# One decoder layer on one core: the order of the queues is made from another simulator's times

## The chip, the core and the metric

The kernel runs on one core of a Trainium2 chip. The metric is the device time of one execution in microseconds (us); the median of three runs is compared. TensorE (PE in the rows) multiplies matrices, VectorE (DVE), ScalarE (ACT) and GpSimd (POOL) do element work, and SyncE (SP) issues most of the DMAs. Each engine works through its own queue of instructions in a fixed order and stops where an instruction's operands are not ready.

## The reference, cut to what matters

1024 prompt positions and 8 single decode positions (1032 columns) go through one layer of width 1024:

```python
h = _rmsnorm(x, p['norm_mix'])
proj = h @ p['w_in']                          # 1024 -> 1792 + 768 + 512 + 3072 columns
z, q, k, v, xq, gates = jnp.split(proj, IN_SPLITS, axis=-1)
out_a, S_new = _rwkv_branch(z, z_prev, S0, p) # a recurrence over the positions
out_b = _sink_attn(...)                       # sliding window, 8 heads
out_c = _mem_attn(xqh, mem_k, mem_v)          # cross-attention, 4 heads
g = jax.nn.sigmoid(gates)                     # three gates of 1024 columns
merged = g0 * (out_a @ w_br_a) + g1 * (out_b @ w_br_b) + g2 * (out_c @ w_br_c)
x = x + merged @ p['w_out']
h2 = _rmsnorm(x, p['norm_ffn'])
x = x + jnp.square(jax.nn.relu(h2 @ p['w_up'])) @ p['w_down']
```

## The kernel before

**Dense products.** All of it is float32. A product is made from high and low parts by three matmuls for each 128 rows of the contraction (`dense`, L181 to L183). `in_proj` computes one block of 128 columns of `proj`: it loads the weights (L163, a tile `wst`), splits them on ACT (L173) and POOL (L174), and runs 24 matmuls into each of three banks named `mm` (384, 384 and 264 columns), 72 in all. ACT takes each bank out. Of these blocks 24 belong to the gates: `gates` puts a tanh on the bank (L286, tile `gt`) and stores it (L287). Below, *a dense matmul* is one of these 128x128 matmuls into an `mm` bank.

**The recurrence** is cut into 8 units, u0 to u7 (`unit`, a generator of three stages). Stage 1 makes the factors of a later unit (among them L479 and L496, small sums on PE). Stage 2 makes the tile `GM` (L545) and solves a triangular system in 62 short DVE operations (L581, L583), 31 after each other. Stage 3 takes the solution (L597, L600) and does four steps, each one a chain across engines: PE L616 and L619, ACT L622, PE L626, ACT L627, PE L629, DVE L631 (the new state), which the next L616 reads. PE's L633 lies beside it. u0 starts its first step at the first L616.

**What stands around the units.** The source puts dense blocks between the stages:

```python
FILL = [lambda: pair_proj(2), lambda: pair_proj(3)] + [lambda i=i: gates((2, 2, 2, 2, 2)[i]) for i in range(5)]
for u in range(7):
    next(units[u + 1])
    if u == 0:
        FILL[0]()
    flush(units[u])
    next(units[u + 1])
    if u:
        FILL[u]()
```

Behind u7 come the cross-attention (16 pieces; first PE row is a `cp` bank from `mkTh`), the keys of the sliding window (L995), 32 pieces of sliding-window attention (`qunit`, L1092 to L1128), the last gates (`gates(24)`, L1257), then the branch products with `w_br_c`, `w_br_a` and `w_br_b` (first row: an `mm` bank from `oh`), the output product, the second norm (about 1345 to 1410 us) and the MLP (`stream`, L1555).

**What sets the order.** The source order is not the queues' order. When the block of the `tile.TileContext` ends, the framework's scheduler goes through the program with a simulator's times, and at each point gives an engine one of the instructions that are ready by those times. Its result is a fixed order for each engine's queue, and with it which tile takes which buffer. Nothing is reordered on the chip by the program itself.

## Time and profile before

| | |
|---|---|
| median of 3 runs | 2059.64 us (2055.43 to 2061.08) |
| the profiled execution | 2062.78 us, its span 2061.0 us |
| mean granted TensorE clock | 0.948 of full speed |
| busy share of the span | PE 94%, PE's weight loads 89%, DVE 65%, ACT 37%, POOL 29% |

The profiled execution is one of its own, beside the three timed runs. The span is from its first to its last instruction. Busy shares are means over stages that have different limits.

### The profile page before, as it was taken

To read this page: it belongs to the slowest core of one execution; us is meant where nothing else is said; L and a number is where in the kernel's file an instruction comes from. 1 tells how busy PE (TensorE), PEld (TensorE's weight loads), DVE (VectorE), ACT (ScalarE), POOL (GpSimd) and SP (SyncE) were. 2 spreads that over 40 slices of the span, in tenths; PEclk is the share of its full clock that TensorE was granted. 3 is DMA by queue.
4 is the path that set the end of the run, shared out by engine and by line. 5 is a ranking of instruction groups with operands and counts; after the bars stand their busy time and mean duration, and the time that the engine had idled before them with its cause. 6 is when DMAs were issued, how large, how long until landed. Compare 5 with 4: busy or idle time off the path is not lost. (4 is left out here: it accounts for less than half of the span.)

```text
span 2061.0 us, 36994 instructions
## 1 busy us (share of the span) xinstructions
PE 1928.9 (94%) x14079; PEld 1834.5 (89%) x14079; DVE 1344.0 (65%) x3247; ACT 755.8 (37%) x1617; POOL 590.7 (29%) x606
## 2 busy tenths in 40 slices
PE   4989999998999989999989999979999998999998
PEld 4879888887888888989979999969999998999997
DVE  7465667576676457477652575687666669788864
ACT  4432323232322335344652123343333344344433
POOL 3422211111111135322020000146655554344421
PEclk9999788799898999999999999989999999999999
DMA  4544322323232145232236346416544448455413
GB/s 142 169 152 130 88 73 80 90 80 93 60 84 70 30 129 168 85 95 79 65 112 212 109 142 206 123 49 197 166 150 137 149 150 288 126 148 159 141 40 101
DMA packets 257104, 250.69 MB, mean 122 GB/s; under 512 B 43102, under 2 KB 204959, under 8 KB 256927
## 3 DMA queue, kind: packets, MB, share of 16 engines
q1 hardware_dynamic: 254656, 241.24, 38.5%
q0 software_dynamic: 2016, 6.53, 1.0%
q8 instruction: 111, 1.82, 0.4%
q14 instruction: 67, 0.54, 0.1%
q10 hardware_dynamic: 254, 0.55, 0.1%
HBM read 174.19 MB, written 74.46 MB: 121 GB/s over the span
## 5 line engine op out<-in xcount | busy, mean ns | idle before, releaser
L181 PE MATMUL mm<-hh,wh 128*128 128x384 f32 (+1 forms) x1152 | 391.7, 340 | 5.7 <-ACT z L342 5.1
L182 PE MATMUL mm<-hl,wh 128*128 128x384 f32 (+1 forms) x1152 | 390.0, 339 | 7.3 <-DVE hl L217 7.3
L183 PE MATMUL mm<-hh,wl 128*128 128x384 f32 (+1 forms) x1152 | 390.5, 339 | 1.3 <-POOL wl L174 1.3
L1555 PE MATMUL z<-h,wl 128*128 128x258 f32 x1488 | 265.6, 287 | 7.9 <-DVE x L1648 4.5
L1555 PE MATMUL z<-h,wh 128*128 128x258 f32 x1488 | 263.2, 285 | 8.1 <-DVE wh L1310 4.9
L182 PEld LDWEIGHTS mm<-hl,wh 128*128 128x128 f32 x1152 | 227.6, 198 | 11.3 <-DVE hl L217 8.2
L181 PEld LDWEIGHTS mm<-hh,wh 128*128 128x128 f32 x1152 | 228.5, 198 | 10.1 <-ACT z L342 5.6
L183 PEld LDWEIGHTS mm<-hh,wl 128*128 128x128 f32 x1152 | 228.3, 198 | 5.1 <-POOL wl L174 1.7
L1555 PEld LDWEIGHTS z<-h,wl 128*128 128x128 f32 x1488 | 217.6, 193 | 9.8 <-ACT wl L1536 5.0
L1555 PEld LDWEIGHTS z<-h,wh 128*128 128x128 f32 x1488 | 216.1, 192 | 9.2 <-DVE wh L1310 5.1
L174 POOL TENSOR_TENSOR wl<-wst,wh 128x1024 fp32r<-128x1024 f32 x48 | 116.9, 2435 | 215.6 <-ACT wh L173 211.1
L1648 DVE TENSOR_TENSOR x<-z,x 128x516 f32<-128x516 f32 x168 | 115.9, 691 | 68.8 <-PE z L1555 65.5
L1555 PE MATMUL z<-l,wl 128*128 128x258 f32 x744 | 154.7, 288 | 3.1 <-DVE l L1310 3.1
L1555 PE MATMUL z<-l,wh 128*128 128x258 f32 x744 | 153.5, 286 | 1.0 <-DVE l L1310 1.0
L173 ACT ACTIVATE wh<-wst 128x1024 fp32r<-128x1024 f32 x84 | 88.8, 1057 | 141.4 <-PE mm L182 75.0
L1555 PEld LDWEIGHTS z<-l,wl 128*128 128x128 f32 x744 | 117.9, 192 | 3.7 <-DVE l L1310 3.6
L1555 PEld LDWEIGHTS z<-l,wh 128*128 128x128 f32 x744 | 117.0, 191 | 1.7 <-DVE l L1310 1.7
L1503 POOL TENSOR_TENSOR sw<-wst 128x256 f32<-128x256 f32 (+1 forms) x56 | 55.1, 984 | 208.0 <-DMA wst<-in_w_down 87.9
L1607 POOL TENSOR_TENSOR us<-us,us 128x516 f32<-128x516 f32 x64 | 96.5, 1519 | 52.0 <-issue 22.1
L1310 DVE TENSOR_TENSOR l<-ub,h 128x516 fp32r<-128x516 f32 (+1 forms) x120 | 92.9, 800 | 6.3 <-ACT h L1335 6.1
L183 PE MATMUL mm<-oh,wl 128*128 128x384 f32 (+1 forms) x288 | 92.2, 320 | 0.0
L182 PE MATMUL mm<-ol,wh 128*128 128x384 f32 (+1 forms) x288 | 92.1, 320 | 0.0
(510 smaller groups left out, 4281.1 us busy)
## 6 DMA issues: line engine op xcount, KB each, us to landing
u<-us SPq DMA_DIRECT2D x112, 258.0 KB
ub<-u SPq DMA_DIRECT2D x112, 258.0 KB
wst<-in_w_in SPq DMA_DIRECT2D x48, 512.0 KB
wst<-in_w_down SPq DMA_DIRECT2D x24, 512.0 KB
gate<-gt SPq DMA_DIRECT2D x48, 192.0 KB
gl<-gate SPq DMA_DIRECT2D x16, 516.0 KB
wst<-in_w_out SPq DMA_DIRECT2D x16, 512.0 KB
wst<-in_w_up SPq DMA_DIRECT2D x16, 512.0 KB
```

The source lines that it names most:

```text
L173: A.activation(hi, st, AF.Copy)
L174: last_lo[:] = [eng.tensor_tensor(lo, st, hi.bitcast(F32), ALU.subtract)]
L181: PE.matmul(out, lhsT=wh, rhs=xh, start=first and k == 0, stop=False)
L182: PE.matmul(out, lhsT=wh, rhs=xl, start=False, stop=False)
L183: end = PE.matmul(out, lhsT=wl, rhs=xh, start=False, stop=last and k == n - 1)
L1310: V.tensor_tensor(lo, x, hi.bitcast(F32), ALU.subtract)
L1503: G.tensor_tensor(s[:, k:k + n], v, w, op)
L1555: op = PE.matmul(z[:, s, :HQ], lhsT=t[:, a, k], rhs=right[ks[k], s, i][b], start=go and k + q == 0, stop=q == 2 and k == nk - 1, skip_grou ...
L1607: G.tensor_tensor(t, x, y, ALU.subtract)
L1648: V.tensor_tensor(c, z, c, ALU.add)
```

## The change

One argument is added where the context is opened. No instruction, operand, pool or line of the kernel's body changes; the framework's scheduler now takes the durations from its other simulator when it orders the queues.

```diff
@@ -1761,7 +1761,7 @@
-    with tile.TileContext(nc) as tc:
+    with tile.TileContext(nc, schedule_with_timeline_sim=True) as tc:
         tile_step(tc, ins, outs)
```

The orders differ over most of the kernel. Three places stand here. The first is PE's queue at the first step of u4. `cp` and `sm` banks belong to the units, `mm` banks are dense blocks. Before:

```order
L616 MATMUL cp_4699<-st_129_601,BR_4037 128x128
L616 MATMUL cp_4699<-st_131_603,BR_4037 128x128
L619 MATMUL cp_4699<-UV_4279,GM_4249 64x64 x4
L183 MATMUL mm_5692<-hh_8_79,wl_5633 128x264
L181 MATMUL mm_5692<-hh_8_79,wh_5632 128x264
L182 MATMUL mm_5692<-hl_9_80,wh_5632 128x264
L183 MATMUL mm_5692<-hh_8_79,wl_5633 128x264
L626 MATMUL cp_4708<-pt_4706,GM_4249 64x64 x4
```

After, at the same step:

```order
L616 MATMUL cp_4699<-st_129_601,BR_4037 128x128
L616 MATMUL cp_4699<-st_131_603,BR_4037 128x128
L619 MATMUL cp_4699<-UV_4279,GM_4249 64x64 x4
L501 MATMUL sm_5262<-c_ident_69,sn_5237 20x128
L626 MATMUL cp_4708<-pt_4706,GM_4249 64x64 x4
L629 MATMUL cp_4708<-UV_4279,CKT_4278 64x64 x4
L633 MATMUL cp_4699<-UV_4279,GM_4249 64x64 x4
L616 MATMUL cp_4727<-st_130_602,BR_4037 128x128
```

The dense matmuls that stood between the step's parts are gone: units u3, u4, u5 and three steps of u6 stand without any. They have moved to earlier units. The second place is PE's queue after the change at the first step of u1:

```order
L600 MATMUL cp_2688<-Y_2676,XW_2480 64x64 x8
L616 MATMUL cp_2700<-st_125_597,BR_1954 128x128
L616 MATMUL cp_2700<-st_127_599,BR_1954 128x128
L619 MATMUL cp_2700<-UV_2460,GM_2430 64x64 x4
L182 MATMUL mm_4522<-hl_7_78,wh_4490 128x384
L183 MATMUL mm_4522<-hh_6_77,wl_4491 128x384
L181 MATMUL mm_4522<-hh_6_77,wh_4490 128x384
```

Of such dense rows 22 follow here before the next row of the step (L626), where three or four stood before the change. Counted over the whole queue, the dense matmuls that stand between two marks are:

| from, to (first row of each) | before | after |
|---|---|---|
| L479 of u0, first step of u0 | 217 | 265 |
| u0, u1 | 138 | 287 |
| u1, u2 | 161 | 306 |
| u2, u3 | 133 | 308 |
| u3, u4 | 157 | 0 |
| u4, u5 | 132 | 0 |
| u5, u6 | 172 | 0 |
| u6, u7 | 93 | 144 |
| u7, first cross-attention row | 323 | 364 |
| cross-attention, L995 | 310 | 209 |
| L995, first `qunit` | 239 | 183 |
| `qunit` pieces and the last gates, to the branch products | 697 | 684 |

Up to the branch products both orders have had the same dense matmuls. Before the first step of u0 the order after has 70 more behind it (22 of them ahead of u0's L479). Nine `qunit` pieces late in their stage have no dense matmul among them after the change, and the last gates stand among the last pieces, where before they stood behind them.

The third place is SP's queue, where the branch products' first weights are loaded. Before:

```order
L287 DMA gate_553<-gt_11464 128x384
L1274 DMA tot_1793_11250<-gate_553 128x1032
L163 DMA wst_11637<-in_w_br_c 128x4x256
L287 DMA gate_553<-gt_11492 128x384
L163 DMA wst_11729<-in_w_br_c 128x4x256
L287 DMA gate_553<-gt_11520 128x264
```

After:

```order
L1274 DMA tot_1794_11251<-gate_553 128x1032
L287 DMA gate_553<-gt_11582 128x384
L163 DMA wst_11637<-in_w_br_c 128x4x256
L163 DMA wst_11729<-in_w_br_c 128x4x256
L287 DMA gate_553<-gt_11610 128x264
L1274 DMA tot_1795_11252<-gate_553 128x1032
```

The load now stands behind four more stores of gate banks; one store of a gate is left behind it, where five were left before. In the MLP the orders are close to each other; loads of `in_w_up` stand behind the loads of `u` there, and the first load of `in_w_out` behind loads of `x`.

## Rows read from the trace of the kernel before

**Rows 1.** The page: busy times; TensorE's clock, in tenths, in 40 slices of the span.

```profile
PE 1928.9 (94%) x14079; PEld 1834.5 (89%) x14079; DVE 1344.0 (65%) x3247; ACT 755.8 (37%) x1617; POOL 590.7 (29%) x606
PEclk9999788799898999999999999989999999999999
```

**Rows 2.** Busy time by stretch: before u0, the qunits, the MLP.

```profile
core 0: us, PE busy (x) PEld busy (x) DVE busy (x) ACT busy (x) POOL busy (x), PEclk, DMA share, GB/s
182.00:281.85 99.85, 87.15 (x514) 80.83 (x513) 67.81 (x196) 27.78 (x54) 20.89 (x30) 0.86 0.36 104
892.00:1115.00 223.00, 208.79 (x1410) 198.21 (x1411) 134.80 (x417) 114.67 (x323) 40.92 (x68) 0.93 0.38 116
1410.00:2061.00 651.00, 635.27 (x5225) 631.45 (x5223) 462.91 (x702) 247.38 (x496) 299.55 (x277) 0.99 0.48 150
```

**Rows 3.** The same for u0 to u7, each from first L616 on, and the cross-attention.

```profile
281.85:339.26 57.41, 56.62 (x394) 49.41 (x393) 40.70 (x149) 18.35 (x45) 8.23 (x10) 0.82 0.28 79
339.26:407.50 68.24, 64.54 (x429) 57.29 (x427) 42.84 (x183) 19.91 (x44) 9.13 (x15) 0.80 0.29 80
407.50:460.43 52.93, 51.37 (x388) 44.32 (x387) 37.80 (x149) 16.66 (x38) 7.26 (x8) 0.90 0.29 79
460.43:523.50 63.07, 57.25 (x419) 49.69 (x417) 41.62 (x173) 19.22 (x43) 7.26 (x8) 0.89 0.31 84
523.50:576.93 53.43, 52.39 (x391) 45.38 (x391) 36.03 (x150) 17.53 (x44) 7.35 (x7) 0.90 0.31 82
576.93:632.48 55.55, 51.26 (x411) 45.86 (x409) 37.52 (x152) 15.12 (x33) 9.01 (x10) 0.94 0.30 81
632.48:668.67 36.19, 35.92 (x294) 31.24 (x293) 25.17 (x107) 12.07 (x26) 5.14 (x4) 0.90 0.19 49
668.67:749.25 80.58, 75.61 (x541) 71.43 (x539) 29.19 (x111) 24.71 (x50) 11.88 (x12) 0.96 0.19 56
749.25:842.70 93.45, 84.55 (x573) 78.68 (x571) 63.19 (x137) 43.69 (x118) 45.30 (x34) 0.98 0.55 165
```

**Rows 4.** The `mm` instructions alone in four of those stretches, and in 1080 to 1110.

```profile
281.85:339.26 57.41, 32.71 (x138) 25.45 (x138) 0.00 (x0) 2.75 (x6) 0.82 0.28 79
460.43:523.50 63.07, 33.13 (x157) 26.49 (x157) 0.00 (x0) 3.23 (x7) 0.89 0.31 84
632.48:668.67 36.19, 20.38 (x93) 14.96 (x93) 0.00 (x0) 3.18 (x7) 0.90 0.19 49
668.67:749.25 80.58, 60.20 (x323) 53.25 (x323) 0.00 (x0) 10.09 (x23) 0.96 0.19 56
...
1080.00:1110.00 30.00, 30.00 (x197) 30.00 (x195) 0.00 (x0) 3.20 (x7) 1.00 0.82 270
```

**Rows 5.** Timeline, the first step of u3: start, duration, engine, line, tiles.

```profile
460.43 0.71 PE L616 MATMUL cp<-st,BR 128*128 128x128 f32 x4
...
463.73 0.45 PE L629 MATMUL cp<-UV,CKT 128*64 128x64 f32 x8
...
464.31 1.18 DVE L631 SCALAR_TENSOR_TENSOR st<-st,gc,cp 64x64 f32<-64x64 f32 x4 [0.62 <-PE cp L629]
```

**Rows 6.** Timeline, the first step of u4.

```profile
523.50 1.22 PE L616 MATMUL cp<-st,BR 128*128 128x128 f32 x4
...
529.91 1.18 DVE L631 SCALAR_TENSOR_TENSOR st<-st,gc,cp 64x64 f32<-64x64 f32 x4 [3.24 <-PE cp L629]
```

**Rows 7.** Waits, 339 to 577 us: total us, times, longest.

```profile
DVE sn L481 <- PE sm L479: 22.5, 4, 6.7
DVE st L631 <- PE cp L629: 13.9, 10, 3.2
DVE xt L581 <- DMA AT<-amat: 7.7, 2, 4.4
```

**Rows 8.** Timeline, SP's first load of `w_br_c` and the first branch row on PE.

```profile
1106.91 0.38 SPq L163 DMA_DIRECT2D wst<-in_w_br_c  x1
...
1119.50 0.33 PE L181 MATMUL mm<-oh,wh 128*128 128x384 f32 x1
```

## The prediction

> **What bounds the kernel now.** I read the page first: PE is busy for 94% of the span and no other engine for more than 65% [rows 1]. So the kernel is PE's queue, and time can come or go in three ways only: dense work, which is the same before and after, stalls of PE, and stretches at the lower clock. The clock line of the page says where to look: the slices at 7 and 8 tenths lie from the first norm to the end of the units [rows 1]. I then cut the span into stages. From 1410 us on PE is busy for 635.27 of 651.00 us at a mean granted clock of 0.99: little to win [rows 2]. The `qunit` stage is busy for 208.79 of 223.00 us, at 0.93 [rows 2]. The units run at 0.80 to 0.94 and PE has idle time in most of them [rows 3].
>
> Third, the price of a dense matmul. Where nothing else runs (1080 to 1110 us, clock 1.00), 197 of them take 30.00 us, 0.152 us each [rows 4]. In u0 PE spends 32.71 us on 138 of them, 0.237 us each, and in the stretch from u7 on 60.20 us on 323, 0.186 us each [rows 4]: beside a recurrence step the same instruction is dearer, since it runs partly at half clock. PE's remaining work in a unit is its busy time less that of the `mm` rows: 56.62 - 32.71 = 23.9 us in u0, 57.25 - 33.13 = 24.1 in u3, and, with no later unit to prepare, 35.92 - 20.38 = 15.5 in u6 and 75.61 - 60.20 = 15.4 in u7 [rows 3, 4].
>
> Fourth, what a step of the recurrence takes. u3's first runs from L616 at 460.43 to the end of L631 at 464.31 + 1.18 = 465.49: 5.06 us, with L616 at 0.71 us for four rows, the level of 2.4 GHz [rows 5]. u4's first runs from 523.50 to 531.09: 7.59 us, and the same four rows take 1.22, the level of 1.2 GHz [rows 6]. DVE follows the chain and solves the next unit's triangle in between: 41.62, 36.03 and 37.52 us busy in u3, u4, u5 [rows 3].
>
> **The change part by part.** The instructions are the same, so every term is an amount of dense work at another place, plus what that place then waits for.
>
> *Before u0.* 70 more dense matmuls stand ahead of u0's first step, 70 x 0.152 = 10.6 us. PE was idle for 99.85 - 87.15 = 12.7 us there, and the clock was 0.86 [rows 2], so that they can fit into gaps: 0, with 0 to +11.
>
> *u0 to u3.* The order now has 287 + 306 + 308 = 901 dense matmuls there, in groups of some 22 between the parts of a step, 3.3 us of cover for a hand-over that needs less. PE should not wait, nor the clock fall: 901 x 0.152 = 137 us, plus 3 x 25 us of its own (24 measured, one for breaks) = 212 us. Before, the three took 57.41 + 68.24 + 52.93 = 178.6 [rows 3]. Term: +33. With own work of 22 us, as it would be wholly at the higher clock, +24; at u7's 0.186 us for a dense matmul, 901 x 0.186 + 75 = 243, +64.
>
> *u3 to u6.* No dense matmul stands there. A unit then takes what DVE and the chain take. Lower bound: DVE's own 38.4 us (the mean of the three), plus its waits in the rows for four units, 13.9 / 4 = 3.5 for L631 and 7.7 / 4 = 1.9 for the loaded triangle, and about 3 of the 22.5 / 4 = 5.6 for L479, which had dense rows ahead of it [rows 7]: 47 us. That holds while the clock is high. At the lower level each of four steps takes 7.59 - 5.06 = 2.53 us more [rows 5, 6], 10 together, and the other PE rows a little: 58 us. The units of before, with three dense rows in a gap, had 0.89, 0.90 and 0.94 [rows 3], so that both levels will occur; I take the middle, 52. u5's recurrence prepares less for what follows, 46. So 52 + 52 + 46 = 150, against 63.07 + 53.43 + 55.55 = 172.1 [rows 3]: -22 (47 gives -37, 58 gives -4).
>
> *u6 to u7.* 51 more dense matmuls, 7.8 us, onto 36.19 [rows 3], so 44; three of the four steps are bare, and at the lower level those add 3 x 2.53 = 7.6, so 51.6. I take 47: +11 (+8 to +15).
>
> *u7 to the cross-attention.* 364 x 0.152 + 15.4 = 70.7 us if nothing waits, against 80.58, of which 16 us were not explained by 323 x 0.152 + 15.4 either [rows 3]. I take half of the gain, -5 (-10 to +6).
>
> *Cross-attention, to L995 and to the first `qunit`.* 101 fewer, 15.4 us of PE in a stretch where PE is busy for 84.55 of 93.45 us [rows 3]; DVE and the loads may then bind, so -11 (-15 to 0). 56 fewer behind it: -8.5 (-8.5 to 0).
>
> *`qunit` pieces.* 13 fewer in all: -2. Nine pieces are bare, the last ones covered; PE's 223.00 - 208.79 = 14 us of gaps [rows 2] can grow or shrink: -4 to +10.
>
> *The first weights of the branches.* Before, the load was issued at 1106.91 and its first matmul ran at 1119.50, 12.6 us later [rows 8]. Now only the last bank of the last gate is left to run after the store ahead of it: 24 x 0.152 = 3.6 us. The load, ACT's and POOL's splitting and SP's queue have 9 us less. How much of the 12.6 was slack, no row says: +7 (0 to +10).
>
> *MLP.* PE's idle time there is 15.7 us in all [rows 2], so today nearly every load is hidden. The few loads that are now queued behind others can open gaps: +4 (0 to as much again, +16).
>
> Sum: 0 + 33 - 22 + 11 - 5 - 11 - 8.5 - 2 + 7 + 4 = +6.5 to +7. Against the profiled execution, 2062.78 us, that is 2069.5; that execution stands 3 us above the median of the three runs, so against 2059.64 it is 2066.5. I forecast **2067 us**. About 0.3% (6 us) is what a measurement of this kernel can tell from no change, and this lies just outside of it.
>
> A look across the terms: dense work is only moved. 129 matmuls more are done by u7 (19.6 us), and those stages come out 22 us longer, the later ones 26.5 shorter before the loads. What remains is a trade, bare units that wait against covered units that don't, and loads that come late.
>
> **The rivals.**
>
> *Faster: bare units keep the higher clock.* Then DVE sets them, at 47, 47 and 41 us (-15), and u6's bare steps cost nothing (-3): 2049 us, and down to 2040 if the covered units come out at 22 us of own work (-9). For it: DVE's rows are continuous there, and PE still has 24 us of work in 47. Against it: u4's first step ran at the lower level although dense rows stood in its gaps [rows 6]. It decides from a bare unit of some 48 us downwards.
>
> *Slower: bare units run at half clock throughout.* 58, 58 and 52 us (+18) and u6 at 51.6 (+4.5): 2089 us. For it: a bare unit leaves PE 24 us of work in some 50, and every stretch of rows 3, all of them fuller, has less than 1.00. Against it: as a mean no stretch went below 0.80 [rows 3], so that the clock rose again each time. It decides from 53 us per bare unit upwards.
>
> The rows show the clock at its lower level in a step whose gaps were not even empty. The Trainium skill ("TensorE: Matmul & The Clock Gate", HAM oscillation) says that a loop whose matmul bursts are shorter than its waits pays the return to the lower clock in every round. By that rule the bare units would be this rival, 2089 us. The Trainium skill ("Perfetto Trace Analysis", Optimization Strategy) also holds that regimes with different limits gain from being interleaved, and this change takes the dense regime out of three units; it speaks for the same rival and names no price.
>
> *Slower: covered units stay as dear as now.* If a dense matmul among recurrence steps costs 0.186 us there as in the stretch from u7 on [rows 4], 901 of them add 901 x 0.034 = 31 us: 2098 us. For it: the weights of 12 blocks must be loaded and split in 212 us while ACT and POOL serve the units. Against it: in 1080 to 1110 us the same chain fed 197 in 30 us [rows 4], 1.5 times the rate that is asked here.
>
> **How the numbers follow.** The forecast, with bare units between 49 and 55 us and the rest near the sum, has 0.38, and by itself would reach from 2052 to 2082. The faster rival has 0.30 (2034 to 2054), half clock 0.22 (2080 to 2100), dear covered units 0.10 (2085 and more). Faster than 2053.5: 0.28 of the rival and 0.05 of the forecast, 0.33. Within 0.3%: 0.02 and 0.15, 0.17. Slower than 2065.8: 0.18, 0.22 and 0.10, 0.50. The range runs from 2034 to 2102; outside lie the lowest of the faster rival and most of the last one, under 0.2.
>
> **What would show it right or wrong.** In the profile after: u0 to u1, u1 to u2 and u2 to u3 should each be near 70 us at a clock of 0.95 or more, with DVE waiting; u3 to u6 near 50 each, PE busy for about half, the clock between 0.6 and 0.8; the cross-attention stretch near 80 us; before the first `mm` row from `oh` a gap on PE of some 7 us that ends at the split of `w_br_c`. Most likely wrong are the price of a bare unit, where 5 us in each move the result by 15, and the assumption that the covered units lose nothing.

## The result

The changed kernel takes 2130.67 us (median of 4 runs, 2126.94 to 2139.24), the kernel before 2057.53 us (median of 4 runs): a ratio of 1.036, 95% interval 1.032 to 1.040. It is 73 us slower, outside of the range of the prediction (2034 to 2102). The profiled execution after took 2126.94 us, the lowest of its four, with a span of 2125.1 us.

The page of the profile after, busy times and clock in 40 slices, answers to [rows 1]:

```profile
PE 1939.0 (91%) x14079; PEld 1858.8 (87%) x14079; DVE 1352.0 (64%) x3247; ACT 756.5 (36%) x1617; POOL 596.7 (28%) x606
...
PEclk9999998999555799999999999998999999999999
```

PE works about as long as before (1939.0 us against 1928.9) in a longer span, and three slices stand at half clock that stood at 8 and 9 tenths. They are the bare units. The windows by stretch after (columns as in [rows 2]): ahead of u0, then u0 to u7, the cross-attention, the `qunit` stage, and the last 652 us of the MLP:

```profile
182.00:280.06 98.06, 90.77 (x593) 87.31 (x591) 62.22 (x152) 26.59 (x51) 23.60 (x31) 0.93 0.41 116
280.06:370.37 90.31, 82.85 (x572) 75.70 (x571) 50.17 (x202) 27.09 (x62) 12.90 (x13) 0.91 0.32 88
370.37:450.57 80.20, 75.94 (x564) 70.94 (x562) 41.99 (x159) 23.29 (x49) 13.73 (x13) 0.94 0.31 84
450.57:530.76 80.19, 75.91 (x564) 70.77 (x562) 43.13 (x165) 21.52 (x45) 12.21 (x11) 0.94 0.31 87
530.76:588.36 57.60, 44.93 (x270) 37.39 (x268) 37.34 (x168) 15.16 (x35) 2.63 (x7) 0.52 0.17 44
588.36:641.40 53.04, 39.51 (x256) 33.21 (x255) 35.19 (x145) 13.94 (x38) 2.60 (x6) 0.56 0.17 44
641.40:698.27 56.87, 37.92 (x241) 31.84 (x241) 36.32 (x159) 10.09 (x24) 4.12 (x8) 0.50 0.17 42
698.27:752.65 54.38, 50.52 (x370) 46.96 (x369) 31.22 (x131) 18.62 (x40) 6.14 (x9) 0.79 0.14 36
752.65:829.36 76.71, 76.71 (x557) 73.36 (x556) 24.37 (x92) 21.24 (x43) 13.41 (x9) 0.98 0.24 73
829.36:910.35 80.99, 70.69 (x464) 66.79 (x464) 61.35 (x134) 39.52 (x110) 43.43 (x33) 0.94 0.56 170
953.35:1171.66 218.31, 199.19 (x1432) 193.11 (x1431) 138.52 (x423) 114.57 (x324) 41.77 (x68) 0.95 0.38 119
1463.00:2115.00 652.00, 638.26 (x5236) 633.80 (x5236) 467.46 (x704) 248.64 (x499) 299.33 (x279) 0.99 0.46 147
```

Against [rows 3], u0, u1 and u2 are longer by 33, 12 and 27 us, and u3, u4 and u5, which no longer hold a dense matmul, are shorter by 5.5, 0.4 and longer by 1.3 us. By the first row of each stretch in both traces:

| stretch | before | after | difference | forecast |
|---|---|---|---|---|
| to u0's first step | 281.9 | 280.1 | -1.8 | 0 |
| u0 to u3 | 178.6 | 250.7 | +72.1 | +33 |
| u3 to u6 | 172.1 | 167.5 | -4.5 | -22 |
| u6 to u7 | 36.2 | 54.4 | +18.2 | +11 |
| u7 to the cross-attention | 80.6 | 76.7 | -3.9 | -5 |
| cross-attention to L995 | 93.4 | 81.0 | -12.4 | -11 |
| L995 to the `qunit` pieces | 49.9 | 43.0 | -6.9 | -8.5 |
| `qunit` pieces and last gates | 227.0 | 218.3 | -8.7 | +5 |
| branch products to the MLP | 233.9 | 234.6 | +0.7 | 0 |
| MLP | 697.6 | 709.0 | +11.4 | +4 |

The differences add up to the 64 us between the two spans; the units alone, u0 to u7, take 472.6 us in place of 386.8, 85.8 more. The `mm` instructions alone in u0, u1 and u2 (columns as in [rows 4]):

```profile
280.06:370.37 90.31, 54.92 (x287) 49.10 (x287) 0.00 (x0) 5.49 (x12) 0.91 0.32 88
370.37:450.57 80.20, 54.86 (x306) 49.97 (x306) 0.00 (x0) 5.96 (x13) 0.94 0.31 84
450.57:530.76 80.19, 52.49 (x308) 48.73 (x308) 0.00 (x0) 4.51 (x10) 0.94 0.31 87
```

The first step of u1 after shows what a group of dense matmuls does there. The timeline, one row of ACT and three of PE:

```profile
371.01 0.68 PE L619 MATMUL cp<-UV,GM 64*64 64x64 f32 x8
...
371.73 0.38 ACT L622 ACTIVATE pt<-cp 64x256 f32<-64x256 f32 x1 [0.49 <-PE cp L619]
...
375.21 0.68 PE L626 MATMUL cp<-pt,GM 64*64 64x64 f32 x8
378.84 0.45 PE L629 MATMUL cp<-UV,CKT 128*64 128x64 f32 x8
```

ACT hands over at 372.11, and PE comes to L626 at 375.21: the chain stands behind the group for 3.1 us, and the second, third and fourth step show the same at this place. What that leaves for the rest of the unit, by the two parts of u1, its steps and what follows (all instructions, then the `mm` ones alone):

```profile
370.37:415.00 44.63, 44.63 (x345) 42.36 (x344) 23.09 (x86) 14.02 (x30) 9.03 (x9) 1.00 0.27 79
415.00:450.57 35.57, 31.32 (x221) 28.58 (x219) 18.90 (x73) 9.28 (x19) 4.70 (x4) 0.86 0.35 90
...
370.37:415.00 44.63, 35.95 (x211) 32.97 (x212) 0.00 (x0) 4.09 (x9) 1.00 0.27 79
415.00:450.57 35.57, 18.91 (x97) 17.00 (x95) 0.00 (x0) 1.86 (x4) 0.86 0.35 90
```

The steps hold 211 dense matmuls with PE never idle; behind them PE waits and the clock falls.

How long a unit's four steps take, from its first L616 to the end of its last L631, tells the two kinds of unit apart. The last L631 of u3 before, then of u0 and of u3 after:

```profile
480.76 1.18 DVE L631 SCALAR_TENSOR_TENSOR st<-st,gc,cp 64x64 f32<-64x64 f32 x4
```

```profile
337.86 1.22 DVE L631 SCALAR_TENSOR_TENSOR st<-st,gc,cp 64x64 f32<-64x64 f32 x4 [7.99 <-issue]
...
560.99 1.18 DVE L631 SCALAR_TENSOR_TENSOR st<-st,gc,cp 64x64 f32<-64x64 f32 x4
```

So the steps of u3 took 21.5 us before and take 31.4 after, without a dense matmul; those of u0 take 59.0. Read in the same way, the steps of u0 to u5 took 21.5 to 26.2 us before; after, u0 to u2 take 59.0, 50.2 and 49.9, and the bare u3 to u5 31.4, 30.5 and 35.0.

### The profile page after: what moved, and what is told of

Read it like the earlier page. It is cut to its first block, busy times and chain, and to the rows that moved or that the text cites. A ratio compares the mean times of both kernels' runs of the same rounds, so it can differ in the third digit from the quotient of the medians.

```text
span 2125.1 us, 37015 instructions
## 1 busy us (share of the span) xinstructions
PE 1939.0 (91%) x14079; PEld 1858.8 (87%) x14079; DVE 1352.0 (64%) x3247; ACT 756.5 (36%) x1617; POOL 596.7 (28%) x606
## 4 chain that ended last, share of the span: by engine, by line
PE 64%; DVE 17%; DMA 10%; issue 4%; ACT 3%; SPq 1%; POOL 1%; DVEq 0%; ACTq 0%; POOLq 0%
PE z L1555 25%; PE mm L183 8%; PE mm L181 8%; PE mm L182 8%; DVE l L1310 3%; DMA AT<-amat 2%; PE z L181 1%; PE z L182 1%; PE z L183 1%; PE cp L616 1%; DMA xmat<-X 1%; DMA ub<-u 1%; DMA xin<-in_x_prompt 1%; PE cp L619 1%; PE cp L626 1%
## 5 line engine op out<-in xcount | busy, mean ns | idle before, releaser
L181 PE MATMUL mm<-hh,wh 128*128 128x384 f32 (+1 forms) x1152 | 382.5, 332 | 13.3 <-ACT z L342 8.1
L182 PE MATMUL mm<-hl,wh 128*128 128x384 f32 (+1 forms) x1152 | 381.6, 331 | 0.0
L183 PE MATMUL mm<-hh,wl 128*128 128x384 f32 (+1 forms) x1152 | 380.3, 331 | 1.0 <-POOL wl L174 1.0
L173 ACT ACTIVATE wh<-wst 128x1024 fp32r<-128x1024 f32 x84 | 89.0, 1059 | 151.6 <-PE mm L182 80.6
L581 DVE TENSOR_TENSOR xt<-X,AT 128x60 f32<-128x60 f32 (+24 forms) x248 | 56.6, 228 | 73.0 <-DMA AT<-amat 67.4
L181 PE MATMUL mm<-oh,wh 128*128 128x384 f32 (+1 forms) x288 | 92.9, 323 | 9.3 <-ACT wh L173 9.3
```

What stands on the lines that cost most here:

```text
L173: A.activation(hi, st, AF.Copy)
L181: PE.matmul(out, lhsT=wh, rhs=xh, start=first and k == 0, stop=False)
L182: PE.matmul(out, lhsT=wh, rhs=xl, start=False, stop=False)
L183: end = PE.matmul(out, lhsT=wl, rhs=xh, start=False, stop=last and k == n - 1)
L581: V.tensor_tensor(o, X[:, 0:r, s:s + 1].to_broadcast([P, r, w]), AT[:, s:s + 1, s + 1:].to_broadcast([P, r, w]), ALU.mult)
```

## The experiments

An order can be bound to an engine: the kernel's end adds an edge of issue order from each instruction to the next in a list. This is the edit of all runs that bind an order; the lists are those of the built programs before or after, or made from them.

```diff
+def follow(tc, engine, packed):
+    order = np.cumsum(np.frombuffer(zlib.decompress(base64.b85decode(packed)), "<i2").astype(np.int64))
+    have = {i.name: i for i in tc.nc.cur_bb.bb.instructions}
+    seq = [have[n] for n in (f"I-{k}" for k in order) if n in have]
+    info = mybir.DependencyInfo(mybir.DependencyClass.NoSync, mybir.DependencyReason.DATA)
+    for a, b in zip(seq, seq[1:]):
+        tc.add_manual_dep(b, a.name, info, reason="order")
...
         tile_step(tc, ins, outs)
+        follow(tc, "PE", ORDER_PE)
```

A run that binds one queue leaves the other four to be ordered anew around it, so that its difference holds what they lose or win as well.

**All five queues bound to the old orders, new times.**

> The changed kernel, whose scheduler is bound to give PE, DVE, ACT, POOL and SP the orders that they had before; only which buffer a tile takes can still come from the new times. If the orders of the queues are the whole change: the time before, 2050 to 2068 us. If the buffers that the new times hand out cost something by themselves: above 2080 us.

2062.67 us, ratio 1.002 (0.997 to 1.007). The orders of the queues are the whole change; what else the new times decide costs nothing that can be measured.

**Only PE bound to its old order, new times; and PE bound to its new order, old times.**

> The changed kernel, whose scheduler is bound to give PE the order that it had before; the other queues are ordered with the new times around it. Theory 1 (the loss is PE's order in the units: a unit takes 53 to 57 us bare or with 150 dense matmuls spread through it, so those taken out of it must be paid elsewhere): near the time before, 2050 to 2068 us. Rival (the new orders of DVE, ACT and the DMA queues cost, as DVE's 34.5 us of waits for the loaded triangle in u0 to u2 suggest): 2095 us or more.

> The kernel before, whose scheduler is bound to give PE the changed kernel's order; the other queues are ordered with the old times around it. Theory 1 (PE's order is the loss): 2118 to 2140 us, units u0 to u3 near 250 us and u3 to u6 near 167. Rival (the other queues' orders): 2080 us or less.

2133.50 us (1.034, 1.029 to 1.039) and 2136.03 us (1.036, 1.032 to 1.041): each is as slow as the change itself. In the first run theory 1 fell, and the rival held (2095 or more); in the second theory 1 held (2118 to 2140), and the rival fell. So neither PE's queue nor the other four are the whole loss. Under the old times PE's new order makes u0 to u7 456.3 us, near the 472.6 of the change, so that the new times for the other queues aren't needed for most of the loss there. With PE's old order and the new times, u0 to u7 takes 419.8 us, and the rest of the loss appears elsewhere: 12 us ahead of u0, 14 at the `qunit` pieces, 13 in the MLP. The waits of PE over u0 to u7, in this run and then in the one with all orders old:

```profile
PE sm L496 <- DVE tmp L494: 21.6, 5, 6.8
PE cp L616 <- DVE st L631: 8.9, 3, 4.2
```

```profile
PE sm L496 <- DVE tmp L494: 6.8, 2, 3.7
```

PE's queue is the same in both; in the first L494 on DVE comes later, and PE stands there. With DVE's old order put back too (the next run), this wait falls to 10.8 us.

**PE and DVE bound to the old orders, new times.**

> The changed kernel, bound to the orders before of PE and DVE only. The run with PE's old order alone stayed at 2133 us, and mostly DVE's order still differed in it. Theory 2a (DVE's order must fit PE's, each alone is as bad as both): 2050 to 2072 us. Rival (what is left of ACT's, POOL's and the DMA queues' orders costs): 2110 us or more.

2081.73 us (1.0095, 1.006 to 1.013): between the two expectations. DVE's old order gives back 52 of the 71 us that PE's old order alone had left; the last 19 us lie with ACT, POOL and the DMA queues. The MLP is back at 696 us.

**The covered units, dense matmuls spread within each.** In u1, from the list (D is a dense matmul):

```
new:    L616 L619 D22 L626 L496 D14 L629 L633 L501 D22 ... L562 D26 L566 ... D10 ... D1 L479 D2 L597 D23 L600
spread: L616 L619 D3 L626 L496 D3 L629 L633 L501 D3 ... L562 D26 L566 D44 ... D89 ... D10 ... D1 L479 D47 L597 D23 L600
```

> The changed kernel's PE order, but in u0, u1 and u2 the dense matmuls that stand in groups of 22 within the four steps are cut to 3 (6 behind a step), and the rest (161, 178 and 178) stands behind the steps, where the triangle of the next unit is solved; each unit keeps its number of dense matmuls. Theory 1 in its form for the covered units (the groups draw the steps out to 41 to 48 us, and the solve behind them is then left without work for PE): u0 to u3 falls from 251 us to 212 to 225, and the whole to 2090 to 2105. Rival (300 dense matmuls in a unit cost what they cost, by their loads, splits and clock, wherever they stand): 2122 to 2135.

2134.40 us (1.034, 1.029 to 1.039): the rival. u0, u1 and u2 take 91.0, 82.2 and 75.0 us; in u2 PE is busy for all of it. In u0 and u1 it is busy for 84.2 and 76.6 us. The steps came out shorter as meant, 40.5, 30.6 and 24.7 us in place of 59.0, 50.2 and 49.9, but the three units together take 248.2 us in place of 250.7: with some 300 dense matmuls a unit takes what PE's work takes, wherever they stand.

**The old order, its dense matmuls packed into the steps of u0 to u5.** In u1:

```
old:    L616 L619 ... D3 L626 ... D3 L629 L633 ... D6 L616 ... L661 D47 L456 ... L479 D35 L496 ... D5 L597 D5 L600
packed: L616 L619 D10 ... D3 L626 D10 ... D3 L629 L633 D10 ... D6 L616 ... L661 L456 ... L479 L496 ... L597 D5 L600
```

> The kernel before's PE order, but in u0 to u5 the dense matmuls that stand behind the steps (77, 107, 85, 105, 84 and 115) are put into the gaps of the four steps, which then hold 10 to 17 each; each unit keeps its number. Theory 1 (placement within a unit counts): the solve is bare and the steps are longer by up to 11 to 16 us a unit, 2110 to 2150 us. Rival (only how many dense matmuls a unit has counts): the time before, 2050 to 2068.

2104.32 us (1.021, 1.015 to 1.027), under the lower end of the theory and far from the rival: the same number in the same unit costs 43 us when it stands in the gaps and the other queues are ordered around it.

**The old order, the steps of u0 to u4 emptied.** The 3 or 4 in each gap go behind L661 and L479.

> The kernel before, PE bound to its own order except that in u0 to u4 the 46 to 54 dense matmuls that stand within the four steps (three or four in a gap) are moved behind the steps, half behind L661 and half behind L479. Theory 3 (three in a gap are hidden by the hand-over between the engines; 244 of them, 38 us, must now be run beside the solve): 2072 to 2095 us. Rival (the steps get shorter by as much): 2052 to 2068.

2117.88 us (1.027, 1.019 to 1.034), more than expected. The windows of u0 to u2 in this run:

```profile
277.38:343.20 65.82, 59.51 (x394) 52.98 (x393) 44.76 (x164) 18.18 (x45) 8.23 (x10) 0.73 0.26 66
343.20:417.18 73.98, 67.33 (x428) 60.36 (x426) 45.90 (x195) 19.98 (x44) 9.11 (x15) 0.73 0.29 74
417.18:483.78 66.60, 59.45 (x387) 53.05 (x386) 41.54 (x175) 17.26 (x38) 7.33 (x8) 0.71 0.25 67
```

The clock is 0.71 to 0.73, where the same units had 0.80 to 0.90 [rows 3]. The last L631 of u0 before, and in this run:

```profile
306.48 1.16 DVE L631 SCALAR_TENSOR_TENSOR st<-st,gc,cp 64x64 f32<-64x64 f32 x4
```

```profile
301.68 1.16 DVE L631 SCALAR_TENSOR_TENSOR st<-st,gc,cp 64x64 f32<-64x64 f32 x4 [1.21 <-PE cp L629]
```

The steps are as long without the dense matmuls as with them, 25.5 us in u0 here and 25.8 before, 24.6 to 27.0 in u0 to u4 here and 21.5 to 26.2 before. So three in a gap made the steps no longer, and the loss lies behind the steps. It is more than the 38 us of work that was moved, and what the rest is, the lower clock or DVE's queue, no run parts: by the order of the starts in the traces, of DVE's 1055 rows from u0's first L631 to u7's first only 195 are at their old place in the sequence here and 152 in the packed run, 133 with PE's old order and the new times, and all 1055 with all five old orders.

**The old scheduler with no gate block in the units.**

```diff
-    FILL = [... gates((2, 2, 2, 2, 2)[i]) for i in range(5)]
+    FILL = [... gates((0, 0, 0, 0, 0)[i]) for i in range(5)]
```

> The kernel before with its old scheduler and no gate block handed to the fillers (0 in place of 2 each); the ten blocks run at the end of the gates. Between the first steps of u0 to u7 stand 138, 113, 0, 0, 0, 0, 35 dense matmuls. It prices a bare unit in the old order, the disputed term. Theory 3 (a unit has a floor of its own near what it takes now, so that some 150 dense matmuls in it are free): u2 to u6 bare take 52 to 58 us each, u0 to u7 stays within 15 us of 387, and the 720 matmuls cost their 0.15 us each at the end: 2150 to 2185 us. Rival (a bare unit of the old order is short, 40 to 47 us): 2110 to 2145 us.

2173.83 us (1.053, 1.046 to 1.059), as theory 3 expected. The windows of u2 to u5, all four without a dense matmul:

```profile
401.86:446.83 44.97, 35.99 (x245) 30.05 (x245) 30.34 (x127) 11.78 (x28) 2.27 (x3) 0.58 0.16 37
446.83:517.63 70.80, 40.16 (x269) 33.67 (x269) 42.52 (x194) 15.42 (x36) 2.77 (x9) 0.57 0.23 53
517.63:567.08 49.45, 42.58 (x256) 35.63 (x255) 30.06 (x125) 13.50 (x37) 2.41 (x4) 0.50 0.14 33
567.08:624.50 57.42, 36.40 (x241) 30.54 (x240) 34.49 (x153) 10.09 (x24) 3.84 (x9) 0.53 0.16 41
```

They average 55.7 us (their single lengths shift with what of the next unit falls into which), and u0 to u7 takes 387.9 us with 700 dense matmuls fewer, against 386.8 with them [rows 3]. The `qunit` stage and the gates behind it take 115 us more for 720. Under the old scheduler the units' usual 93 to 172 dense matmuls are free.

**The old scheduler with uneven gate blocks** (4, 4, 2, 0, 0 in the same line).

> The kernel before with its old scheduler, its gate blocks handed to the fillers as 4, 4, 2, 0, 0 in place of 2 each: between the first steps of u3, u4, u5, u6, u7 stand 288, 246, 33 and 64 dense matmuls in place of 157, 132, 172 and 93; nothing else of the source changes. Theory 2b (a unit takes the larger of a floor of 53 to 57 us, set by its chain, and PE's work, so that up to 150 dense matmuls in it are free, and uneven shares lose): u3 and u4 at 72 to 82 us, u5 not under 50, the whole at 2075 to 2092. Rival (a dense matmul costs the same wherever it stands): 2050 to 2068.

2103.26 us (1.020, 1.014 to 1.026), slower by more than expected. The windows of u3 to u5, with 288, 246 and 33 dense matmuls:

```profile
434.18:513.46 79.28, 75.38 (x549) 68.43 (x547) 45.23 (x152) 22.44 (x49) 12.57 (x10) 0.94 0.29 83
513.46:599.48 86.02, 77.99 (x532) 69.98 (x531) 51.04 (x184) 23.93 (x54) 12.40 (x15) 0.86 0.30 86
599.48:679.58 80.10, 53.23 (x323) 45.00 (x322) 42.48 (x187) 15.18 (x37) 5.48 (x10) 0.56 0.14 36
```

Uneven shares lose under the old scheduler as well; u5 with 33 is not shorter for them, but longer, at a clock of 0.56.

**The new times with more gate blocks** (2, 2, 4, 4, 4).

> The changed kernel with four more gate blocks handed to the fillers (2, 2, 4, 4, 4 in place of 2 each): 310 dense matmuls now stand in u3, 120 in u4, none in u5, and 304 fewer at the `qunit` pieces. Theory 2b (the bare units have room): u3 goes from 57.6 to about 80, u4 stays within 5 us of 53, and the matmuls taken from the end save 0.157 us each, some 48 us; with what else moves 2085 to 2110. Rival (the pieces at the end lose their cover, or dense matmuls cost their price in the units too): 2120 to 2140.

2127.43 us (1.031, 1.026 to 1.037): the rival, nearly no gain. u3 goes to 83.5 us as expected. u4 with 120 dense matmuls takes 63.8 us, 10.8 more than bare: 0.09 us for each, so that they are not free there.

**The new times with paced fillers.**

```diff
+                firsts.setdefault(u, op)   # op: the unit's first L616
...
         if u:
-            FILL[u]()
+            with tc.issue_after(firsts[u - 1].ins):
+                FILL[u]()
```

> The changed kernel with one more rule for its scheduler: the dense matmuls of the filler behind unit u may not stand ahead of the first step of unit u - 1 on PE. Between the first steps of u0 to u7 stand 216, 144, 144, 144, 144, 288 and 132 dense matmuls (before 138, 161, 133, 157, 132, 172, 93; with the change 287, 306, 308, 0, 0, 0, 144), and 888 ahead of u0 (997, 1067). All orders still come from the new times. Theory 2c (two thirds of the loss are the uneven shares: PE idle and at half clock in the bare units, over-full in the others): u0 to u7 falls from 472 us to 390 to 425, the whole to 2065 to 2095. Rival (the loss is how the new times order DVE against PE, as in the run with PE's old order, wherever the dense matmuls stand): 2110 to 2140.

2137.37 us (1.038, 1.033 to 1.042): the rival. u1 to u4, with 144 each, take 69.5, 72.7, 72.2 and 67.5 us. The shares are even, but in u1 all 144 stand in seven gaps of the first three steps again, 15 to 22 in each.

**Paced, and spread in the unit, under the new times; and the same PE order with the old times for the other queues.** The groups in the gaps are cut to 3, the rest stands beside the solve, as above.

> The paced kernel (even shares of dense matmuls, new times), with PE bound to its order except that within u0 to u5 the groups in the steps' gaps are cut to 3 (6 behind a step) and the rest stands beside the solve. Even shares alone (2137 us) and spreading alone (2134) each gave nothing. Theory 4 (dense matmuls are hidden only where they are both even over the units and spread in them): u0 to u7 falls from 494 us by 35 to 60, the whole to 2075 to 2105. Rival (the order of DVE and the rest by the new times sets the units' time whatever PE does): 2120 to 2145.

> The same PE order, instruction for instruction, with DVE, ACT, POOL and the DMA queues ordered by the old times. Theory 4 with what the run with PE's and DVE's old orders showed (DVE's new order costs beside it, some 20 to 50 us in all): 2040 to 2085 us, and below the other kernel of this call by 15 or more. Rival (with PE's order given, the other queues' times don't matter): within 10 us of it.

2139.53 us (1.036, 1.032 to 1.039) and 2146.82 us (1.041, 1.035 to 1.048). Both rivals held, and theory 4 fell. u1 to u4 of the first take 67.7, 67.3, 74.0 and 58.6 us, on the mean 3.6 less than paced alone, and u0 and u5, whose shares were still 216 and 288, take 82.5 and 87.6.

**Both orders joined.** PE and DVE follow the old order to the end of u7's steps, the new one to the branch products, then the old one again.

> The kernel before, its scheduler bound on PE and DVE to a joined order: the order of before up to the end of u7's steps, the changed kernel's order from there to the branch products, the order of before behind them. With the change the stretch from u7 to the branch products took 419 us in place of 451, of which 129 dense matmuls that it had done earlier are 20. If the new order is better there by itself: 12 us under the time before, 2044 to 2054. Rival (it was faster only because its dense work was done before): 2056 to 2070.

2061.77 us (0.9985, 0.9958 to 1.0012): no difference, the rival. u7 to the branch products takes 450 us, as before. Of the 32 us that the change saved there, 20 are the 129 dense matmuls that it had done earlier, at 0.152 us each; the other 12 did not come with the orders of PE and DVE alone. No run here beats the kernel before.

## Why the prediction was wrong

The price of a unit, by the dense matmuls in it, is what the runs add up to (us from first step to first step; means where several are given):

| dense matmuls in the unit | 0 | 120 to 172 | 246 to 310 |
|---|---|---|---|
| orders before, or the old scheduler | 55.7 (4 units) | 58.6 (u1 to u5) | 79.3, 86.0 |
| orders by the new times | 55.8 (u3 to u5), 53.8 | 63.8; 70.5 (paced); 66.9 (paced, spread) | 90.3, 80.2, 80.2, 83.5 |

Single units lie far off these means, since rows of the next unit fall into one or the other: under the old scheduler with uneven gate blocks u5 took 80.1 us with 33 dense matmuls and 290 rows of its own on PE, and u2 40.0 with 96 and 201. The three terms of the units were 64 us too low in all, the other terms together 6 too high.

**The covered units** (+33 forecast, +72 measured): the step that failed is "PE should not wait, nor the clock fall". The three units took 80 to 90 us at a granted clock of 0.91 to 0.94, not some 70 at 0.95 or more. Dense matmuls took 162 us there, where 901 x 0.152 = 137 was put; PE's own rows took 72, where 75 was put; and PE was idle for 16 us (250.7 less 234.7 busy), where nothing was put. So the price of the rival "covered units stay as dear as now" was the right one, at 0.180 us each over the three units, near its 0.186; it had a chance of 0.10. The reason that the working gave for that price, "since it runs partly at half clock", is at most a part of it: in u1's steps, at a clock of 1.00, a dense matmul took 35.95 / 211 = 0.170 us, and behind them, at 0.86, 18.91 / 97 = 0.195. The term's upper end, +64, was passed because it had only the dear matmuls and not the idle time. The longest waits of PE from 280 to 531 us stand ahead of L597, which takes the solution:

```profile
PE cp L597 <- issue: 8.0, 2, 4.3
PE cp L597 <- DVE bv L665: 4.3, 1, 4.3
```

DVE, which makes this solution, waits longer for the loaded triangle than before, by the first row below over the same stretch, and by the second over u0 to u2 before (281 to 461 us). That this is what holds L597 up was not tested.

```profile
DVE xt L581 <- DMA AT<-amat: 34.5, 4, 10.8
```

```profile
DVE xt L581 <- DMA AT<-amat: 3.4, 1, 3.4
```

**The bare units** (-22 forecast, -4.5 measured): the step that failed is "I take the middle, 52". Their lower bound of 47 needed the clock, and the granted clock was 0.50 to 0.56 through all three, below the 0.6 to 0.8 that was expected. The other bound, 58, 58 and 52 us, adds to 168; measured are 57.6, 53.0 and 56.9, 167.5. The rival "bare units run at half clock throughout" was right in the sum, by luck to the microsecond, since its errors in u4 and u5 are 5 us each and cancel; its reason is borne out by the steps, 9 us longer per unit than before, where it put 10. u6 at 54.4 lies beyond its 51.6. The rule of the Trainium skill ("TensorE: Matmul & The Clock Gate", HAM oscillation) pointed to this outcome. Its condition, bursts shorter than the waits between them, is not what this trace shows, taken over a unit: PE is busy for 44.93, 39.51 and 37.92 us of these three, more than half of each.

Where the dense work of these units went can be read off. The `mm` rows of u4 and u5 before, beside those of u3 in [rows 4]:

```profile
523.50:576.93 53.43, 28.44 (x132) 21.85 (x132) 0.00 (x0) 2.25 (x5) 0.90 0.31 82
576.93:632.48 55.55, 32.14 (x172) 27.12 (x172) 0.00 (x0) 3.23 (x7) 0.94 0.30 81
```

PE lost 93.7 us of dense rows in the three units. Its own rows grew from 67.2 to 122.4 us, at 0.50 to 0.56 of the clock in place of 0.89 to 0.94, and its idle time from 11.2 to 45.2. Of the 93.7 us that leaves 4.5.

**The two as rivals.** I gave the two slow cases chances side by side, as if only one could come, and both came: +22 and +31 on 2067 make 2120. The working had already seen that 461 dense matmuls, 70 us at 0.152, would free no more than 22 us in u3 to u5, and it charged their full price in u0 to u2 without asking why. The measured answer is starker: taking them out made the three units 4.5 us shorter, and 700 taken out under the old scheduler changed u0 to u7 by 1 us. A bare unit at half clock takes as long as one with some 150 dense matmuls at 0.80 to 0.94. What a bare unit would take at the full clock, no run shows. The Trainium skill's advice to interleave regimes with different limits ("Perfetto Trace Analysis", Optimization Strategy) speaks of this, and names no price; undoing it cost here 85.8 us in the units, which hold 59 dense matmuls (9 us) more than before.

**What I then held, and what fell.** That the groups of 22 are the loss fell for the covered units (spread, they take the same). For units with the usual share it is open: packed they lose 43 us, with the steps emptied 57, but DVE's queue changed with PE's in both runs. That even shares would give the time back fell too: under the new times a unit with 144 costs 67 to 71 us on the mean, spread or not. What stands is that the loss is the orders of the queues, and PE's and DVE's above all: with PE's old order alone 71 us of loss are left, with PE's and DVE's 20, with all five none, and PE's new order under the old times loses 75. DVE's queue was not exchanged by itself, and no run moved dense matmuls among the units with DVE's queue held. Which of a unit's small instructions makes the remaining 8 us at equal shares was not found; the old times for the other queues beside a PE order that was made under the new ones didn't help (2146.82 us).

**The late weights** (+7 forecast): PE waits once ahead of the branch products, by the waits from 1142 to 1173 us after:

```profile
PE mm L181 <- ACT wh L173: 9.3, 1, 9.3
```

The place and the cause, the split of `w_br_c`, were right, and 9.3 us lie in the range given. The pieces ahead of it came out some 18 us shorter in place of 2, so that the stretch shows -8.7; 14 of the 18 are PE's busy time, 213.3 us before and 199.2 after, and why it fell so far stays open. **The MLP** (+4 forecast, +11.4): the range held it, the reason did not. With DVE's queue by the new times the MLP took 709.0 us (the change) and 711 (PE's old order alone); with PE's and DVE's old orders it took 695.8, though SP's queue was still ordered by the new times. But SP's queue came nearer to its old order too in that run, and with PE's new order and the old times for DVE and SP the MLP still took 705.8, against 695.8 to 701.2 in the runs that had PE's and DVE's old orders there. So the three queues were not parted. **The other stretches** (0, -5, -11, -8.5) came out at -1.8, -3.9, -12.4 and -6.9.

## What to carry to other kernels

Before costing work that is moved, ask what the place that it leaves would take without it: here units with none and with some 150 dense matmuls took the same 56 to 59 us, so that moving them saved next to nothing and cost their full price elsewhere. Two rivals that can both come true belong in one sum. The orders of two queues that hand work to each other are better judged together: PE's replaced alone, the old one among new ones or the new one among old ones, cost as much as the whole change.

## What the runs showed of the hardware that was not expected

PE can be busy for most of the time and run at half clock: the bare units were granted 0.50 to 0.56, and PE was busy in them for 44.93 of 57.60, 39.51 of 53.04 and 37.92 of 56.87 us. And the same work at another place in a unit changed the clock: with three dense matmuls taken out of each gap and run behind the steps, units that PE still filled for 59 to 67 us ran at 0.71 to 0.73 in place of 0.80 to 0.90.
